# One of the two softmax rows per four that TensorE turned goes through a DMA turn: window attention heads of a hybrid encoder layer

## Chip, cores and metric

The kernel runs on one core of a Trainium2 chip. The metric is the device time of one execution in microseconds (us). The time before is 1037.27 us, the median of 3 runs (1036.99 to 1037.58).

## What is computed

One encoder layer over 1024 tokens of width 1024, in float32. One normed input feeds one projection; eight "A" heads do sliding-window attention with a learned sink, eight "B" heads do neighbourhood attention on a 16 x 64 grid; both are normed, joined and projected out; then a gated MLP and a last norm. The change is in the A heads alone, whose core in the reference is, per block of 128 queries and a span of 384 keys:

```
s = einsum('bqgrd,bkgd->bgrqk', q_i, k_i) * scale
s = where(valid, s, -1e30)
m = maximum(max(s, axis=-1), sink_gr)
p = exp(s - m[..., None])
denom = sum(p, axis=-1) + exp(sink_gr - m)
o = einsum('bgrqk,bkgd->bgrqd', p, v_i) / denom[..., None]
```

There are 2 key/value heads (g) with 4 query heads each (j = 0 to 3) and 8 query blocks (b).

## The kernel before

**Stages.** The projections of the input are made as jobs: each is a chain of products of 128x512 (L172, L173, L174: high part by high, low by high, high by low). While the first jobs run, their q, k and v are split into high and low parts and stacked. Then attention runs as 48 units, 16 for the A heads (two g times eight b, `unit_window`) and 32 for the B heads (`units_grid`). The remaining jobs are poured in between as filler, so TensorE always has products to do beside the attention. After attention come the output projection and the MLP.

**A softmax row.** "Row" here is the 128 queries of one block of one head, with 256 keys at the two ends of the sequence and 384 elsewhere. It goes through `Rows.softmax`: GpSimd copies the sink beside the scores (L461), VectorE adds the mask, moves the scores out of PSUM and finds the maximum (L462), ScalarE takes the exponential and the sum (L466), VectorE the reciprocal (L467). After that the row must be split into a high and a low float16 part and turned, because the product with v (L521) needs keys on the partitions. A letter of `PATH_A` says how, for j = 0, 1, 2, 3:

- D: ScalarE writes the high part (L481) and VectorE the low part (L483) into a staging buffer, and a DMA on SyncE's queue turns both at once (L488).
- P: GpSimd scales the row (L470), ScalarE writes the high part (L476), GpSimd subtracts for the low part (L477), and the same DMA turns both (L488).
- T: GpSimd scales the row (L470), TensorE turns it in blocks of 128x128 into a PSUM bank named pt (L494), ScalarE copies the high part out of that bank (L497) and VectorE makes the low part from it (L498).

`PATH_A` was "DPTT". The staging buffers are three, `hl` and two pieces of `stage`, taken in turn (`staged`). A T row stays in its `p` buffer, of which there are five, until TensorE turns it; the bank pt has two buffers. The turned rows of two heads share one `Rows` tile, and the six products of a unit with v (L521) read first the tile of j = 0 and 1, then that of j = 2 and 3.

**What sets the order.** TensorE's order is written by hand: in unit u the scores of unit u + 2 (L432), the products of unit u with v (L521) and the turns of the T rows of unit u + 1 (L494) form one list of events. `T_NEXT` says at which places of that list the turns are put in, `T_AT` does so for the T rows of unit 0, and `T_B` for the B heads. Behind every event the filler is given a share of its rate divided by the number of events, `per = RATES[wi] / (8 if u < 16 else 4) / len(events)`; the shares are summed as a float in `debt`, and `fill(int(debt))` pours in so many steps of filler. The other engines' orders come from a scheduler that works from priorities.

Of the kernel before, what the change touches and what calls it, by code (L numbers as in the profile page):

```python
# [37 lines left out]
TURNED, PS, HLS, SPARE_A, LOWS = 3, 5, 1, (2, 5), 1  # L38
LEAD = 3
BIAS0, YS = 8, 1  # L40
T_AT = (0, 4)
PATH_A, PATH_B = "DPTT", ["QQTQQQTQ"] * 8
T_B, T_NEXT = (0, 3), (3,8)
SPARE_B = [(1, 3), (1, 3), (3,), ()]
WARM = 10

# [17 lines left out]
def hybrid_layer(tc, xT, w_in, w_out, w_gate, w_up, w_down, small, sink, rpb, consts, rope, out):  # L64
    nc = tc.nc
    with ExitStack() as ctx:
# [890 lines left out]
        for u in range(len(flat)):  # L957
# [8 lines left out]
            if u == 0:  # L966
                for i, w in enumerate(flat[u][4]):
                    events.insert(T_AT[i], ("v", w))
            if u + 1 < len(flat):
# [918 lines left out]
```

## Time and profile before

| | |
|---|---|
| median of 3 runs | 1037.27 us |
| span of the profiled execution, first to last instruction | 1035.9 us |
| what the median has beyond that span | 1.3 us |
| TensorE busy | 1011.7 us (98%) |
| VectorE, ScalarE, GpSimd busy | 880.0, 679.3, 214.1 us |
| window attention on TensorE, about | 62 to 191 us |
| grid attention, about | 191 to 350 us |

Times in rows are in us from the span's start. A row of the timeline has the start, the duration, the engine, the line and the operation; what stands in brackets is how long the engine had been idle ahead of it, and who released it. PE is TensorE, PEld its loading of weights, DVE VectorE, ACT ScalarE, POOL GpSimd, SPq the queue of SyncE. The time before one execution's first instruction and behind its last is not in the trace; the table takes it as the difference of median and span.

### The profile page before, as it was taken

What the parts mean: (1) busy time and instruction counts of PE and PEld (TensorE: products, weight loads), DVE (VectorE), ACT (ScalarE), POOL (GpSimd) and SP (SyncE); (2) the same over time, 40 slices, a digit from 0 to 9 for tenths busy, and PEclk for the clock granted to TensorE, in tenths of its full rate; (3) what the DMA queues carried; (4) which work ended last, traced back from release to release, by engine and by line L of the source; (5) the groups of instructions that cost most, each with busy time, mean ns of one, the idle gap of its engine ahead of it and who ended that gap; (6) DMA issues with size and microseconds to landing.
All of it is one profiled execution on the core that took longest, in us unless ns stands there. A gap on an engine that the chain in (4) does not pass through costs nothing.

```text
span 1035.9 us, 15696 instructions
## 1 busy us (share of the span) xinstructions
PE 1011.7 (98%) x5102; PEld 577.3 (56%) x5102; DVE 880.0 (85%) x1748; ACT 679.3 (66%) x1243; POOL 214.1 (21%) x341
## 2 busy tenths in 40 slices
PE   9998999999999999999999999999999999999996
PEld 7776777777775545544444444444444444444446
DVE  6699998766898699899898988888888879899875
ACT  8567787767687587645777777754535656655551
POOL 2235455676866301000000000000000000000002
PEclk9999999999999999999999999999999999999998
DMA  9447473676689775300687867733232778878744
GB/s 347 155 98 149 109 139 83 151 168 140 134 180 224 213 276 193 121 1 21 222 266 261 276 241 250 251 111 133 82 112 102 240 252 297 301 250 264 255 153 163
DMA packets 144275, 191.28 MB, mean 185 GB/s; under 512 B 77376, under 2 KB 88640, under 8 KB 144192
## 3 DMA queue, kind: packets, MB, share of 16 engines
q1 hardware_dynamic: 133536, 164.51, 54.7%
q10 hardware_dynamic: 10656, 25.76, 6.4%
q8 instruction: 40, 0.66, 0.2%
q14 instruction: 43, 0.35, 0.1%
HBM read 132.81 MB, written 28.57 MB: 156 GB/s over the span
## 4 chain that ended last, share of the span: by engine, by line
PE 71%; DVE 6%; ACT 1%; DMA 1%; issue 1%; POOL 0%; ACTq 0%; DVEq 0%; SPq 0%; POOLq 0%
PE dn L1177 6%; PE dn L1178 6%; PE dn L1176 6%; PE pj L180 6%; PE z L1176 5%; PE z L1177 5%; PE z L1178 5%; PE y L1176 4%; PE y L1177 4%; PE y L1178 4%; PE x L1176 4%; PE x L1177 4%; PE x L1178 3%; PE pj L172 2%; PE pj L174 2%; PE pj L173 2%
## 5 line engine op out<-in xcount | busy, mean ns | idle before, releaser
L1178 PEld LDWEIGHTS <-wlo 128*128 128x128 f16 x898 | 87.9, 98 | 101.3 <-DVE wlo L1151 0.2
L1176 PEld LDWEIGHTS <-whi 128*128 128x128 f16 x898 | 88.1, 98 | 100.3
L1177 PEld LDWEIGHTS <-whi 128*128 128x128 f16 x898 | 87.9, 98 | 100.3 <-issue 0.2
L1178 PE MATMUL dn<-xd,wlo 128*128 128x512 f16 (+1 forms) x330 | 120.4, 365 | 0.0
L1177 PE MATMUL dn<-xd,whi 128*128 128x512 f16 (+1 forms) x330 | 120.4, 365 | 0.0
L1176 PE MATMUL dn<-xd,whi 128*128 128x512 f16 (+1 forms) x330 | 120.4, 365 | 0.0
L172 PE MATMUL pj<-xgh,whi 128*128 128x512 f32 x248 | 106.8, 431 | 0.8 <-ACT whi L156 0.8
L1177 PE MATMUL z<-hg,whi 128*128 128x512 f16 x264 | 100.1, 379 | 0.0
L1178 PE MATMUL z<-hg,wlo 128*128 128x512 f16 x264 | 100.1, 379 | 0.0
L1176 PE MATMUL z<-hg,whi 128*128 128x512 f16 x264 | 100.1, 379 | 0.0
L466 ACT ACTIVATE p<-p,nm 128x385 f32<-128x385 f32 (+3 forms) x128 | 74.8, 585 | 38.0 <-DVE nm L462 33.3
L174 PE MATMUL pj<-xgh,wlo 128*128 128x512 f32 x248 | 97.9, 395 | 1.4 <-POOL wlo L157 1.4
L173 PE MATMUL pj<-xgl,whi 128*128 128x512 f32 x248 | 97.5, 393 | 0.0
L1150 ACT ACTIVATE whi<-ws,m 128x512 f16<-128x512 f32 (+1 forms) x96 | 65.9, 709 | 35.6 <-DVE ws L1317 19.5
L1151 DVE SCALAR_TENSOR_TENSOR wlo<-ws,m,whi 128x512 f16<-128x512 f32 (+1 forms) x96 | 70.2, 741 | 17.8 <-ACT whi L1150 17.6
L1031 POOL TENSOR_TENSOR back<-back,cst 128x4 f32<-128x4 f32 (+1 forms) x7 | 2.8, 396 | 356.7 <-DVE back L1030 356.7
L1165 ACT ACTIVATE scan<-scan 128x1024 f32<-128x1024 f32 (+1 forms) x60 | 61.1, 1019 | 17.0 <-DMA scan<-in_w_down_dram 12.3
L1150 ACT ACTIVATE whi<-raw,m 128x512 f16<-128x512 f32 (+1 forms) x78 | 51.4, 700 | 17.9 <-DMA raw<-in_w_down_dram 12.7
L1151 DVE SCALAR_TENSOR_TENSOR wlo<-raw,m,whi 128x512 f16<-128x512 f32 (+1 forms) x78 | 55.4, 732 | 7.5 <-ACT whi L1150 6.9
L1176 PE MATMUL y<-hg,whi 128*128 128x512 f16 x160 | 60.6, 379 | 0.0
L1177 PE MATMUL y<-hg,whi 128*128 128x512 f16 x160 | 60.6, 379 | 0.0
L1178 PE MATMUL y<-hg,wlo 128*128 128x512 f16 x160 | 60.6, 379 | 0.0
(291 smaller groups left out, 2465.5 us busy)
## 6 DMA issues: line engine op xcount, KB each, us to landing
xd<-x SPq DMA_DIRECT2D x77, 256.0 KB, 5.4
raw<-in_w_down_dram SPq DMA_DIRECT2D x64, 256.0 KB, 3.8
x<-c ACTq DMA_DIRECT2D x22, 512.0 KB, 3.5
scan<-in_w_gate_dram SPq DMA_DIRECT2D x18, 512.0 KB, 4.7
scan<-in_w_up_dram SPq DMA_DIRECT2D x18, 512.0 KB, 4.3
raw<-in_w_gate_dram SPq DMA_DIRECT2D x18, 512.0 KB, 3.8
raw<-in_w_up_dram SPq DMA_DIRECT2D x18, 512.0 KB, 4.4
raw<-in_w_in_dram SPq DMA_DIRECT2D x32, 256.0 KB, 3.1
```

The costliest lines, as they stand in the source:

```text
L172: nc.tensor.matmul(ps, w[0], x[0][:, tsl(h)], start=first, stop=False)
L173: nc.tensor.matmul(ps, w[0], x[1][:, tsl(h)], start=False, stop=False)
L174: nc.tensor.matmul(ps, w[1], x[0][:, tsl(h)], start=False, stop=last)
L180: nc.tensor.matmul(ps, a, b, start=i == 0 and b is x[h][0] and a is w[0], stop=i == len(ws) - 1 and a is w[1])
L466: nc.scalar.activation(p[:, 0:e], p[:, 0:e], AF.Exp, bias=nm, scale=-1.0, accum_out=sm)
L1031: nc.gpsimd.tensor_tensor(back, back, unit_back.to_broadcast([128, n]), op=ALU.mult)
L1150: mark["whi"] = nc.scalar.activation(hi, src, AF.Copy, scale=by)
L1151: nc.vector.scalar_tensor_tensor(lo, src, by, hi, op0=ALU.mult, op1=ALU.subtract)
L1165: nc.scalar.activation(t, t, AF.Square, accum_out=dst)
L1176: nc.tensor.matmul(ps, w[0], x[0], start=first and i == 0, stop=False, skip_group_check=True)
L1177: nc.tensor.matmul(ps, w[0], x[1], start=False, stop=False, skip_group_check=True)
L1178: nc.tensor.matmul(ps, w[1], x[0], start=False, stop=last and i == len(ws) - 1, skip_group_check=True)
```

## The change

Head j = 2 goes the way of P in place of T, and the tables of places lose the entry of the turn that is gone. The constants feed every unit of the A heads; nothing else is edited.

```diff
-T_AT = (0, 4)
-PATH_A, PATH_B = "DPTT", ["QQTQQQTQ"] * 8
-T_B, T_NEXT = (0, 3), (3,8)
+T_AT = (4,)
+PATH_A, PATH_B = "DPPT", ["QQTQQQTQ"] * 8
+T_B, T_NEXT = (0, 3), (8,)
```

TensorE, at the first unit of the A heads, before; pt is the bank a row is turned into, p the row, o the output, s the scores, pj a projection.

```order
L494 MATMUL pt_855<-cst_89,p_765 128x128 x3
L521 LDWEIGHTS v_466
L521 MATMUL o_833<-turned_610,v_466 128x256
L521 LDWEIGHTS v_466
L521 MATMUL o_833<-turned_610,v_466 128x256
L172 MATMUL pj_783<-xgh_281,whi_701 128x512
L173 MATMUL pj_783<-xgl_282,whi_701 128x512
L174 MATMUL pj_783<-xgh_281,wlo_702 128x512
L494 MATMUL pt_866<-cst_89,p_671 128x128 x2
L432 MATMUL s_871<-ka_538,q_545 128x384
```

The same place on TensorE now.

```order
L521 LDWEIGHTS v_466
L521 MATMUL o_834<-turned_610,v_466 128x256
L521 LDWEIGHTS v_466
L521 MATMUL o_834<-turned_610,v_466 128x256
L432 MATMUL s_858<-ka_538,q_545 128x384
L432 MATMUL s_858<-kb_539,q_545 128x384
L172 MATMUL pj_789<-xgh_281,whi_704 128x512
L173 MATMUL pj_789<-xgl_282,whi_704 128x512
L174 MATMUL pj_789<-xgh_281,wlo_705 128x512
L494 MATMUL pt_875<-cst_89,p_674 128x128 x2
```

The turn of the next unit's j = 2 (p_765) is gone; the turn of this unit's j = 3 (p_671, now p_674) is left, and it stands behind the scores that it stood ahead of.

GpSimd over the same rows, before; hl and stage are the staging buffers.

```order
L470 TENSOR_SCALAR p_652<-p_652,sm_654 128x256
L470 TENSOR_SCALAR p_671<-p_671,sm_673 128x256
L364 COPY up_727<-up_727 64x1
L350 TENSOR_TENSOR gains_121<-par_79,up_727 128x1 x2
L461 COPY p_793<-nsink_168 128x1
L470 TENSOR_SCALAR p_714<-p_714,sm_716 128x384
L477 TENSOR_TENSOR hl_622<-p_714,hl_622 128x3x128
```

GpSimd now.

```order
L470 TENSOR_SCALAR p_652<-p_652,sm_654 128x256
L470 TENSOR_SCALAR p_674<-p_674,sm_676 128x256
L477 TENSOR_TENSOR stage_621<-p_652,stage_621 128x2x128
L461 COPY p_799<-nsink_168 128x1
L364 COPY up_730<-up_730 64x1
L350 TENSOR_TENSOR gains_121<-par_79,up_730 128x1 x2
L461 COPY p_841<-nsink_168 128x1
L470 TENSOR_SCALAR p_717<-p_717,sm_719 128x384
L477 TENSOR_TENSOR stage_621<-p_717,stage_621 128x3x128
```

The subtraction for j = 2 (p_652) has come in between, and the copies, scalings and subtractions of the following rows stand behind it. SyncE's queue has one more L488 per unit, between the loads of weights and the moves of q, k and v.

TensorE in the B heads, late (a turn of the sixth head), before; mg is the normed mix that the output projection reads.

```order
L180 LDWEIGHTS whi
L180 MATMUL pj<-mg,whi 128x512
L180 LDWEIGHTS whi
L180 MATMUL pj<-mg,whi 128x512
L180 LDWEIGHTS wlo
L180 MATMUL pj<-mg,wlo 128x512
L494 MATMUL pt<-cst,p 128x128 x3
L596 LDWEIGHTS v
L596 MATMUL o<-turned,v 128x256
```

The same turn now.

```order
L494 MATMUL pt<-cst,p 128x128 x3
L180 LDWEIGHTS whi
L180 MATMUL pj<-mg,whi 128x512
L180 LDWEIGHTS whi
L180 MATMUL pj<-mg,whi 128x512
L180 LDWEIGHTS wlo
L180 MATMUL pj<-mg,wlo 128x512
L596 LDWEIGHTS v
L596 MATMUL o<-turned,v 128x256
```

One step of filler (three products) has passed from ahead of the turn to behind it. Nothing of the B heads is edited: the sum in `debt` now comes from eleven events a unit where there were twelve, it lands on the other side of a whole number, and the step comes out one event later. The same stands at some other turns of the later B heads.

## The prediction

> **What bounds the kernel now.** I read the page's busy times first, then the table by stage, then what ended last.
>
> ```profile
> PE 1011.7 (98%) x5102; PEld 577.3 (56%) x5102; DVE 880.0 (85%) x1748; ACT 679.3 (66%) x1243; POOL 214.1 (21%) x341
> PEclk9999999999999999999999999999999999999998
> PE 71%; DVE 6%; ACT 1%; DMA 1%; issue 1%; POOL 0%; ACTq 0%; DVEq 0%; SPq 0%; POOLq 0%
> core 0: us, PE busy (x) PEld busy (x) DVE busy (x) ACT busy (x) POOL busy (x), PEclk, DMA share, GB/s
> 76.00:191.00 115.00, 110.27 (x631) 82.79 (x629) 104.08 (x347) 88.46 (x226) 57.04 (x120) 1.00 0.60 123
> 191.00:350.00 159.00, 155.34 (x877) 114.33 (x877) 121.64 (x359) 115.05 (x256) 114.63 (x144) 1.00 0.78 161
> ```
>
> TensorE is busy 98% of the span at a full granted clock, and the chain that ended last is mostly its own. In the window attention (the row 76:191) it is busy 110.3 of 115 us. But VectorE is close behind with 104.1 us, ScalarE has 88.5, GpSimd only 57.0, and the DMA engines are busy six tenths of it. So in this stage TensorE's work and its waits set the time, VectorE has about 10% of room, and what the change hands to GpSimd and DMA lands where there is room. After this stage TensorE's order is full of products to the end, so what it gains here should pass through.
>
> **What the removed turn costs TensorE.** Matmuls overlap, so their durations say too much; I take the starts.
>
> ```profile
> 97.67 0.39 PE L174 MATMUL pj<-xgh,wlo 128*128 128x512 f32 x1
> 97.90 0.33 PE L432 MATMUL s<-ka,q 128*128 128x384 f32 x1
> 98.07 0.34 PE L432 MATMUL s<-kb,q 128*128 128x384 f32 x1
> 98.95 0.40 PE L174 MATMUL pj<-xgh,wlo 128*128 128x512 f32 x1
> 99.18 0.49 PE L494 MATMUL pt<-cst,p 128*128 128x128 f32 x3
> 99.43 0.42 PE L432 MATMUL s<-ka,q 128*128 128x384 f32 x1
> 99.69 0.34 PE L432 MATMUL s<-kb,q 128*128 128x384 f32 x1
> 125.42 0.38 PE L494 MATMUL pt<-cst,p 128*128 128x128 f32 x2
> 125.56 0.36 PE L432 MATMUL s<-ka,q 128*128 128x256 f32 x1
> ```
>
> Without a turn the scores start 0.23 us after the product ahead of them (97.67 to 97.90), and the second score matmul 0.17 later. With three turned blocks in between it is 0.48 (98.95 to 99.43) and 0.26: the turn takes 0.25 us and makes the next matmul 0.09 later, 0.34 together. Two blocks take 0.14 (125.42 to 125.56), with the same 0.09 some 0.23. There are 16 turns less, 12 of three blocks and 4 of two (the ends of the sequence, twice): 12 x 0.34 + 4 x 0.23 = 5.0 us. If the 0.09 is hidden, it is 12 x 0.25 + 4 x 0.14 = 3.6.
>
> **The waits ahead of the turns.** In the window attention the turns are also where TensorE stands still.
>
> ```profile
> L494 PE MATMUL pt<-cst,p 128*128 128x128 f32 x88 | 15.2, 277 | 3.7 <-DVE turned L498 1.3 <-POOL p L470 1.3 <-POOL p L461 1.1
> 80.19 0.44 PE L494 MATMUL pt<-cst,p 128*128 128x128 f32 x2 [1.31 <-DVE turned L498]
> 95.56 0.52 PE L494 MATMUL pt<-cst,p 128*128 128x128 f32 x3 [1.08 <-POOL p L461]
> 118.20 0.55 PE L494 MATMUL pt<-cst,p 128*128 128x128 f32 x3 [0.34 <-POOL p L470]
> 163.10 0.55 PE L494 MATMUL pt<-cst,p 128*128 128x128 f32 x3 [0.41 <-POOL p L470]
> 179.69 0.55 PE L494 MATMUL pt<-cst,p 128*128 128x128 f32 x3 [0.52 <-POOL p L470]
> ```
>
> The five sum to the 3.7 us of the group. Turns alternate between j = 2 and j = 3; by their order, the last four are all j = 2, the turn that goes. They waited for GpSimd's scaling of that row. The first (80.19) is j = 3 of the first unit, waiting for VectorE to empty the bank pt; two turns of j = 2 had just filled both banks, and these go as well. So I take off all 3.7 us, with 0 as the other bound if the next thing is as late.
>
> What is late next would be the turn of j = 3. It had room:
>
> ```profile
> 148.12 0.59 POOL L470 TENSOR_SCALAR p<-p,sm 128x384 f32<-128x384 f32 x1
> 150.87 0.49 PE L494 MATMUL pt<-cst,p 128*128 128x128 f32 x3
> L477 POOL TENSOR_TENSOR stage<-p,stage 128x384 f16<-128x384 f32 x8 | 7.4, 920 | 2.3 <-ACT stage L476 2.1
> L477 POOL TENSOR_TENSOR stage<-p,stage 128x256 f16<-128x256 f32 x3 | 2.0, 675 | 0.5 <-ACT stage L476 0.5
> ```
>
> Its row was ready 2.2 us before its turn (148.71 to 150.87). GpSimd now has one subtraction more per unit, 0.92 us, on the same queue and ahead of this row's scaling in most units, so the row is later by about that; and TensorE comes sooner. On the other side the turn itself stands one event later. I let this row wait as the other did in steady units: 1.08 + 0.34 + 0.41 + 0.52 = 2.35 us of new waits. The bounds are 0 and 16 x 0.92 = 14.7.
>
> **What moves to other engines.**
>
> ```profile
> L498 DVE TENSOR_TENSOR turned<-pt,turned 128x384 f16<-128x384 f32 x24 | 13.0, 553 | 2.2 <-ACT turned L497 2.0
> L497 ACT ACTIVATE turned<-pt 128x384 f16<-128x384 f32 x24 | 11.2, 480 | 0.6 <-PE pt L494 0.5
> L476 ACT ACTIVATE stage<-p 128x384 f16<-128x384 f32 x8 | 4.2, 525 | 3.3 <-POOL p L470 3.2
> L461 POOL COPY p<-nsink 128x1 f32<-128x1 f32 x59 | 16.2, 278 | 33.3 <-PE pt L494 15.2 <-DVE stage L483 9.8 <-DVE hl L483 7.3
> L488 SPq DMA_TRANSPOSE turned<-stage x21: 1198/1222/1922, 67.6 to 185.6; - x21
> turned<-stage SPq DMA_TRANSPOSE x21, 2.8
> ```
>
> None of these is on the path while TensorE has work. VectorE loses 16 subtractions of up to 0.553 us, at most 8.8 us. ScalarE trades a copy of 0.480 for one of 0.525: 16 x 0.045 = 0.7 us more. GpSimd gains 12 x 0.92 + 4 x 0.675 = 13.7 us. If the stage shrinks by some 7 us to 108, the shares are VectorE 95.3 / 108 = 88%, ScalarE 89.2 / 108 = 83%, GpSimd 70.7 / 108 = 65%: no engine overtakes TensorE. The p buffer of j = 2 is freed sooner: GpSimd stood 15.2 us in front of L461 because TensorE had not yet turned a row; that works for the change. SyncE's queue issues 16 turns more at 1.22 us, 19.5 us, and each lands 2.8 us after its issue. Its order puts them ahead of loads of weights and moves of q, k and v; a unit takes about 7.5 us, a row of unit u + 2 is made during unit u, so this row has two units (15 us) until its product. Cost: nothing, as long as that cover holds. On the other DMA side, a load that comes one turn (1.2 us) later is still a whole job ahead.
>
> **The later turns.** The order of filler around some turns of the B heads moves by one step of three products, and one such turn already waited:
>
> ```profile
> 312.64 0.38 PE L180 MATMUL pj<-mg,wlo 128*128 128x512 f16 x1
> 314.04 0.55 PE L494 MATMUL pt<-cst,p 128*128 128x128 f32 x3 [1.02 <-POOL p L470]
> 311.99 0.38 PE L180 MATMUL pj<-mg,wlo 128*128 128x512 f16 x1
> ```
>
> A step is 0.65 us (311.99 to 312.64). This turn now comes that much sooner for a row that GpSimd is not done with: +0.65. The other turns that move had no wait; bounds: 0, and 7 x 0.65 = 4.6 if all seven that I count lacked room.
>
> **The sum**, against the profiled span of 1035.9 us: -5.0 (turns) - 3.7 (waits) + 2.35 (new waits) + 0.65 (B heads) = -5.7, so 1030.2. The median of the runs is 1.3 above that span, so I forecast 1031.5 us.
>
> **Rivals.**
>
> *No new waits (0.16).* The free p buffers and the idler VectorE bring every row sooner, and j = 3 keeps its room. Then -5.0 - 3.7 + 0.65 and nothing else: 1029.2; with a similar gain at the B heads' turns instead of the loss, 1028.
>
> *GpSimd's queue becomes late (0.14).* If the subtraction delays each remaining turn by half its 0.92 us, the new waits are 16 x 0.46 = 7.4 in place of 2.35: 1036.5. For it: j = 2 had four waits on this engine. Against: GpSimd at 65%, and the 2.2 us of room. It decides when the row of j = 3 is later by over 2.2 us.
>
> *VectorE becomes the bound (0.06).*
>
> ```profile
> 74.81 1.11 POOL L477 TENSOR_TENSOR hl<-p,hl 128x384 f16<-128x384 f32 x1 [0.64 <-ACT hl L476]
> 75.05 1.42 DVE L157 TENSOR_TENSOR wlo<-raw,whi 128x512 fp32r<-128x512 f32 x1
> L157 DVE TENSOR_TENSOR wlo<-raw,whi 128x512 fp32r<-128x512 f32 x11 | 8.3, 754 | 0.1
> ```
>
> Beside a GpSimd subtraction VectorE's split of weights took 1.42 us where the mean is 0.754. If each of the 16 new subtractions costs VectorE 0.67 us, that is 10.7, more than the 8.8 it loses; the stage stays near 106 us of VectorE work and nothing is gained: about 1037. [...]
>
> *Slower: the DMA turn is the slow way (0.12).*
>
> ```profile
> 74.20 0.53 ACT L476 ACTIVATE hl<-p 128x384 f16<-128x384 f32 x1 [1.39 <-POOL p L470]
> 75.95 1.21 SPq L488 DMA_TRANSPOSE turned<-hl  x1
> ```
>
> Three rows per unit now share three staging buffers, so each buffer must be written, subtracted, issued and read within one unit. In these rows that takes from 74.20 to 75.95 and 2.8 more, 4.6 us, of a unit that shrinks to about 7. If SyncE's queue, which issues in order, adds over 2.4 us, ScalarE stands in front of a full buffer with the next rows' exponentials behind it, and TensorE runs out of rows. One us lost in each of the 14 later units gives 1037.3 - 5.0 - 3.7 + 0.65 + 14 = 1043.2. Against it: no wait for a staging buffer in the window attention before. [...]
>
> **Chances and range.** Forecast 0.50, the rivals 0.16, 0.14, 0.06 and 0.12, the rest (0.02) unknown. About 0.2% (2 us) is what a measurement of this kernel can tell from no change. Faster by more: the forecast, the first rival and the milder part of the second (0.10): 0.76. Within it: the rest of the second, the third, and a little: 0.12. Slower: 0.12. The range goes from the first rival (1028.0) over the forecast to the second and third (1037.3), and leaves out the slow case.
>
> **What would show it.** In the profile after: 44 L494 of the window attention instead of 88; the idle time ahead of them at 1 to 3 us; unit spacing near 7.1 us; GpSimd's idle time for TensorE ahead of L461 halved; no ScalarE wait for a DMA at L476 or L481. I am wrong if TensorE waits at L521 for a DMA, if L494 waits for L470 in most units, or if the B heads' turns give back more than 2 us.

## The result, and the profile after

The kernel with the change takes 1040.66 us (median of 8 runs, 1038.42 to 1043.57), the kernel before on the same chip 1037.67 (8 runs, 1036.83 to 1038.82): a ratio of 1.0025, interval 1.0014 to 1.0036. It is slower by some 2.6 us, where 6 us less were forecast, and it lies outside the range (1028.0 to 1037.3). The profiled execution took 1043.35 us, one of the longest of the eight, with a span of 1041.6 against 1035.9 before.

To see in which stage the time goes, I take three marks on TensorE in both profiles: the first scores (start of the window attention), the first and the last product of the B heads. These are the rows of the kernel before, then of the kernel after.

```profile
62.29 0.28 PE L432 MATMUL s<-ka,q 128*128 128x256 f32 x1
197.53 0.39 PE L596 MATMUL o<-turned,v 128*128 128x256 f16 x2
353.05 0.38 PE L596 MATMUL o<-turned,v 128*128 128x256 f16 x2
```

```profile
64.92 0.28 PE L432 MATMUL s<-ka,q 128*128 128x256 f32 x1
199.61 0.27 PE L596 MATMUL o<-turned,v 128*128 128x256 f16 x1 [0.27 <-DMA turned<-stage]
356.79 0.27 PE L596 MATMUL o<-turned,v 128*128 128x256 f16 x1
```

The window attention went from 135.24 to 134.69 us, half a microsecond less where 6.4 were forecast (all of the sum but the B heads' 0.65). The B heads went from 155.52 to 157.18. The rest of the 5.7 us is ahead of the attention (2.6) and behind the B heads (2.0). TensorE's order is the same ahead of the first scores; other profiles of this study, with that order too, have them between 62.13 and 63.81, so I take most of the 2.6 for scatter between executions, and judge by medians below. The profile after shows where it lies: near 20 us TensorE waits 1.76 us ahead of L172 where it waited 0.56 before, and behind that the granted clock is 0.83, 0.50 and 0.81 in three stretches of 2 us, 1.7 us of work lost. None of the other 18 profiles has a slow clock there.

The clock is no small part of the medians either. The mean granted clock of an execution was 0.992 to 0.995 after (the eight runs, middle value 0.993) and 0.995 to 0.998 before (26 runs beside e1 to e4, middle value between 0.996 and 0.997). Over the span that is an estimated 7.3 us lost after and 3.6 before, from clocks given to a thousandth, which is 1 us: as much as the whole difference of the medians, or more.

In the window attention, the turns did what was said: fewer of them, and no wait ahead of them. The groups at the turn and at the product with v, for the stage 76 to 191 us, after; the row of L521 before follows, since it was not shown.

```profile
L494 PE MATMUL pt<-cst,p 128*128 128x128 f32 x42 | 7.2, 278 | 0.0
L521 PE MATMUL o<-turned,v 128*128 128x256 f16 x162 | 30.4, 279 | 6.5 <-ACT turned L497 4.0 <-DVE mixa L536 2.4 <-DVE turned L498 0.2
```

```profile
L521 PE MATMUL o<-turned,v 128*128 128x256 f16 x165 | 30.7, 277 | 0.9 <-DVE mixa L536 0.6 <-DVE by L480 0.2
```

The stage's row after, for VectorE's share:

```profile
76.00:191.00 115.00, 107.89 (x589) 80.48 (x587) 98.79 (x330) 88.69 (x225) 70.56 (x135) 0.99 0.76 144
```

VectorE is busy 98.8 of 115 us, 86%. It has less to do than before (104.1), near the 88% that was expected, and yet, as the rows below show, it is what TensorE waits for.

Ahead of the turns TensorE no longer stands at all: 3.7 us before, 0.0 now. But it stands 6.5 us ahead of L521 where it stood 0.9. The largest of these waits is in the first unit. TensorE, then VectorE, then ScalarE, and the table by 2 us behind it:

```profile
80.96 0.38 PE L494 MATMUL pt<-cst,p 128*128 128x128 f32 x2
85.31 0.27 PE L521 MATMUL o<-turned,v 128*128 128x256 f16 x1 [3.98 <-ACT turned L497]
```

```profile
81.18 1.82 DVE L375 SCALAR_TENSOR_TENSOR vhl<-t,down,vhl 64x1024 f16<-64x1024 f32 x1
83.03 0.62 DVE L462 CUSTOM_DVE_ANT_0 p<-s,cst,nsink 128x384 f32<-128x384 f32 x1
```

```profile
83.69 0.62 ACT L466 ACTIVATE p<-p,nm 128x385 f32<-128x385 f32 x1 [2.98 <-DVE nm L462]
84.90 0.36 ACT L497 ACTIVATE turned<-pt 128x256 f16<-128x256 f32 x1
```

```profile
core 0: us, PE busy (x) PEld busy (x) DVE busy (x) ACT busy (x) POOL busy (x), PEclk, DMA share, GB/s
82.00:84.00 2.00, 0.00 (x0) 0.00 (x0) 1.97 (x4) 0.31 (x1) 1.16 (x2) 1.00 0.80 194
84.00:86.00 2.00, 0.50 (x3) 0.32 (x3) 1.53 (x8) 1.94 (x7) 0.59 (x1) 1.00 0.86 131
86.00:88.00 2.00, 2.00 (x9) 1.39 (x8) 0.71 (x2) 0.44 (x1) 1.17 (x3) 0.54 0.53 109
88.00:90.00 2.00, 2.00 (x9) 1.56 (x9) 1.14 (x5) 1.07 (x4) 0.01 (x1) 0.60 0.88 87
```

The releaser that the row names, ScalarE's copy L497, is not the cause. It was ready to run at 81.3, but stood on ScalarE's queue behind exponentials (L466) that waited for VectorE's maximum (L462), and this stood on VectorE's queue behind the split of v (L375, 1.82 us; 1.28 in the same place before). So the lateness was handed on from queue to queue: the wait of 3.98 us is named after the last link, and its root, the 1.82 us of L375, is two engines back. Behind it the granted clock was 0.54 and 0.60 for 4 us, another 1.7 us of work lost (2 x 0.46 + 2 x 0.40). The last section has shorter stands behind which the clock fell too.

So the stage adds up: -5.0 (turns) - 3.7 (waits at the turns) + 5.6 (waits at L521) + 1.7 (clock) = -1.4, against -0.55 measured. With 0.4 us of waits at L432 and the 0.27 ahead of the first L596 it is -0.7.

In the B heads the moved step is at 314 us in the profile before, here at 318. TensorE, GpSimd, and the table by 2 us:

```profile
313.98 0.38 PE L180 MATMUL pj<-mg,wlo 128*128 128x512 f16 x1
317.92 0.58 PE L494 MATMUL pt<-cst,p 128*128 128x128 f32 x3 [3.56 <-POOL p L470]
```

```profile
313.78 1.43 POOL L554 TENSOR_TENSOR xb<-cst,rr 128x384 f32<-128x384 f32 x1
...
316.31 1.55 POOL L470 TENSOR_SCALAR p<-p,sm 128x384 f32<-128x384 f32 x1
```

```profile
318.00:320.00 2.00, 2.00 (x8) 1.02 (x9) 0.94 (x2) 1.39 (x3) 1.74 (x4) 0.57 1.07 278
320.00:322.00 2.00, 2.00 (x9) 1.19 (x8) 0.28 (x1) 0.00 (x0) 1.82 (x3) 0.58 1.02 135
```

The turn waits 3.56 us instead of 1.02, on a GpSimd that makes the next head's bias (L554, and L555 behind it) ahead of the scaling (L470), and again TensorE runs at 0.57 and 0.58 for 4 us behind it.

### The profile page after: what moved, and what is told of

It is laid out like the page before. It is cut to its first block, busy times and chain, and to the rows that moved or that the text cites. A ratio compares the mean times of both kernels' runs of the same rounds, so it can differ in the third digit from the quotient of the medians.

```text
span 1041.6 us, 15641 instructions
## 1 busy us (share of the span) xinstructions
PE 1011.6 (97%) x5058; PEld 575.2 (55%) x5058; DVE 873.3 (84%) x1732; ACT 678.6 (65%) x1243; POOL 229.0 (22%) x357
## 4 chain that ended last, share of the span: by engine, by line
PE 60%; DVE 10%; DMA 6%; ACT 3%; issue 3%; POOL 1%; SPq 0%; DVEq 0%; ACTq 0%; POOLq 0%
PE pj L180 8%; PE z L1176 5%; PE z L1177 5%; PE z L1178 5%; PE x L1176 3%; PE y L1176 3%; PE x L1177 3%; PE y L1177 3%; PE y L1178 3%; PE x L1178 3%; DMA xd<-x 2%; PE dn L1177 2%; PE dn L1176 2%; PE dn L1178 2%; DVE xd L1581 2%
## 5 line engine op out<-in xcount | busy, mean ns | idle before, releaser
L172 PE MATMUL pj<-xgh,whi 128*128 128x512 f32 x248 | 108.2, 436 | 0.6 <-ACT whi L156 0.6
L174 PE MATMUL pj<-xgh,wlo 128*128 128x512 f32 x248 | 98.5, 397 | 1.4 <-POOL wlo L157 1.4
L466 ACT ACTIVATE p<-p,nm 128x385 f32<-128x385 f32 (+3 forms) x128 | 74.8, 585 | 31.3 <-DVE nm L462 30.2
```

The costliest lines, as they stand in the source:

```text
L172: nc.tensor.matmul(ps, w[0], x[0][:, tsl(h)], start=first, stop=False)
L174: nc.tensor.matmul(ps, w[1], x[0][:, tsl(h)], start=False, stop=last)
L466: nc.scalar.activation(p[:, 0:e], p[:, 0:e], AF.Exp, bias=nm, scale=-1.0, accum_out=sm)
```

## The experiments

Every ratio is against the kernel before, timed on the same chip beside it. The experiments ran on four chips, a question at a time, so kernels of different questions are compared by their ratios. Waits come from the one profile of a kernel, and one execution is not the median: e3's is the fastest of its twelve.

**First question: which part costs?** One edit moves the first turn of j = 3 back by one event, away from its own product; another gives the sum `debt` the value that it has in the kernel before, so that TensorE's order in the B heads is that of before.

e1, the turn alone:

```diff
-T_AT = (4,)
+T_AT = (3,)
```

> The changed kernel with the first unit's one turn put one event earlier (place 3 in place of 4), so that a product step and the scores stand between the turn and the product that reads it. Theory 1 (the loss is two stalls: the first unit's turn stands right ahead of its own product, and the moved filler step in the B heads): the wait of 4.2 us at L521 near 81 us falls under 1 us and the slow clock of 0.54 to 0.60 behind it (about 1.7 us lost) goes, so 5 to 6 us less than the changed kernel: 1034.5 to 1036. Rival (the way over GpSimd and DMA is itself slower, the place does not matter): about 1040.7, as the changed kernel.

Measured: 1043.15 us, ratio 1.0046 (1.0032 to 1.0060).

e2, the order of the B heads alone:

```diff
-            wi = u // 8 if u < 16 else 2 + (u - 16) // 4
+            wi = u // 8 if u < 16 else 2 + (u - 16) // 4; debt = 0.9999999999999971 if u == 16 else debt
```

> The changed kernel with the filler's carried sum set at the first unit of the B heads to the value that the kernel before has there, so that TensorE's order in the B heads is that of before. Theory 1: the wait at the turn near 314 us falls from 3.7 to about 1.2 us and the slow clock behind it goes (1.7 us): about 4 us less than the changed kernel, 1036.5. Rival (A heads only): within 1 us of 1040.7.

Measured: 1038.80 us, ratio 1.0004 (0.9994 to 1.0013).

e3, both edits:

> Both edits of the two kernels ahead of this one. Theory 1: the gains add, 9 to 10 us less than the changed kernel: 1031 to 1032, the sum of the prediction. Rival (GpSimd and DMA way is slower): 1038 to 1041, not faster than the kernel before.

Measured: 1039.40 us, ratio 1.0018 (1.0007 to 1.0028).

e4, the kernel before with the B heads' order of the kernel after:

```diff
-            wi = u // 8 if u < 16 else 2 + (u - 16) // 4
+            wi = u // 8 if u < 16 else 2 + (u - 16) // 4; debt = 0.9999999999999949 if u == 16 else debt
```

> The kernel before, its filler's carried sum set at the first unit of the B heads to the value of the changed kernel, so that only the order in the B heads is the changed one. Theory 1: slower than before by 0.65 us (the step alone) to 4 us (if the wait passes the length at which the clock falls): 1038.3 to 1041.7. Rival (the late row in the B heads came from what the change does upstream): 1037.7, as before.

Measured: 1041.15 us, ratio 1.0029 (1.0018 to 1.0040). Its wait at that turn is 3.54 us, for the same L470, and the granted clock behind it 0.63 and 0.51 in two stretches of 2 us (318 to 322 us). The 4 us of the expectation suppose a length of wait at which the clock falls; no run shows a fixed one (last section).

e2 and e4 agree: the step that a rounding moved in the B heads is worth 2 to 3 us (0.0021 between after and e2, 0.0029 between e4 and before). With it out of the way, the change in the window attention is worth nothing (e2: 1.0004), not 6 us. The theory on the first turn's place fell: in e3 that wait became shorter (2.58 us in place of 3.98), and the kernel no faster (e1 1.0046 against 1.0025 after, e3 1.0018 against 1.0004 in e2). The waits came back further on. TensorE's waits in e3, 62 to 200 us (engine, tile, line waited for: us in total, times, longest):

```profile
PE o L521 <- DVE mixa L536: 4.6, 3, 2.6
PE o L521 <- DVE turned L498: 2.8, 2, 2.6
PE s L432 <- DVE nm L462: 1.3, 3, 0.6
```

VectorE is named in every one of them. One of the waits for mixa, the emptying of the o bank: TensorE, ScalarE, then VectorE's queue.

```profile
95.05 0.39 PE L521 MATMUL o<-turned,v 128*128 128x256 f16 x2 [2.56 <-DVE mixa L536]
```

```profile
89.27 0.38 ACT L532 ACTIVATE ot<-o 64x256 f32<-64x256 f32 x1
```

```profile
89.28 1.22 DVE L341 TENSOR_TENSOR kb<-t,ka 64x1024 fp32r<-64x1024 f32 x1
90.42 0.60 DVE L483 SCALAR_TENSOR_TENSOR hl<-p,by,hl 128x384 f16<-128x384 f32 x1
...
91.58 0.55 DVE L498 TENSOR_TENSOR turned<-pt,turned 128x384 f16<-128x384 f32 x1
92.05 0.68 DVE L269 TENSOR_TENSOR t<-pj,rstd 128x512 f32<-128x512 f32 x1
92.64 1.22 DVE L299 SCALAR_TENSOR_TENSOR t<-t,q 128x1024 fp32r<-128x1024 f32 x1
...
94.49 0.50 DVE L536 TENSOR_TENSOR mixa<-o,ot 64x128 f32<-64x128 f32 x2
```

ScalarE's half of the bank was done at 89.65, and no row of VectorE between 89.28 and 94.49 has a wait: L536 stood 4.8 us behind other work. Theory 2: VectorE, which takes its work in the order of its queue, is as late as TensorE, so what TensorE saves it waits for VectorE. Rival: GpSimd's added subtractions, by their queue or by contention (in the profile after an L157 on VectorE took 1.41 us beside GpSimd's L477, the median of eleven is 0.683).

**Second question: VectorE or GpSimd?** e5 moves the low part of the weights (L157) from VectorE to GpSimd; e6 does it to the kernel before; e7 leaves out GpSimd's new subtraction; e8 gives it to VectorE.

e5, on e3:

```diff
-            if u == 12:
+            if u == 0:
                 mark["attention"] = True
```

> The kernel of e3 (j = 3 turned one event earlier, B heads' filler in the old order; its median was 1039.4 us), and from the first attention unit on the low part of the weights (L157) is made by GpSimd, where before that starts with the thirteenth unit. That takes some 11 operations of 0.75 to 0.88 us, 8 to 10 us, off VectorE in the window attention and gives GpSimd about as much. Theory (VectorE's in-order queue is as late as TensorE in the window attention, so that what TensorE saves it waits at the products with v, L521, and the scores, L432): VectorE's results come sooner, TensorE's waits at L521 for VectorE's mixa (L536) and turned (L498) shrink from the 5 to 6 us of e3 to 2 to 3, and the median is 1033 to 1036. Rival (GpSimd's queue and its contention with VectorE eat the gain): GpSimd, at 70.6 of 115 us after the change, gets later still, two-input VectorE work is slowed more, and the median is 1040 to 1045, with waits for POOL in the place of those for VectorE.

Measured: 1042.51 us, ratio 1.0037 (1.0022 to 1.0051).

e6, the same edit on the kernel before:

> The kernel before with the same move of the weights' low part (L157) to GpSimd from the first unit, as control for e5. Theory (VectorE late): before the change TensorE's waits in the window attention were 6.3 us in large ones, 4.1 of them the first turn and GpSimd's; VectorE has most of its late work in the first three units, so the move helps before as well, but less than after: 1035.5 to 1038. Rival (GpSimd late): GpSimd's scaling, which the turns of j = 2 waited for, comes later, and the median is 1039 to 1043.

Measured: 1038.11 us, ratio 0.9996 (0.9986 to 1.0006).

e7, on e3 (j counts within a pair of rows here, so that the one meant is j = 2; the buffers are cleared once ahead):

```diff
-                        nc.gpsimd.tensor_tensor(lo, x, hi, op=ALU.subtract)
+                        if j: nc.gpsimd.tensor_tensor(lo, x, hi, op=ALU.subtract)
```

> The kernel of e3 with the low part of the DMA-turned row of j = 2 left out: GpSimd's subtraction L477 for that row is not made (the three staging buffers are set to zero once), so that the row's low part is not that of the reference. 16 GpSimd operations of 0.68 to 0.92 us, 13.7 us, are gone, with all their contention; VectorE keeps all its work. Theory (VectorE's own queue): VectorE's operations in the window attention get 1.6 us shorter at most (what e3 showed them to be longer by), and the median is 1037.5 to 1039.5, little better than e3 (1039.4). Rival (GpSimd's subtractions eat the gain, by its queue or by contention): the whole gain that was forecast comes back, 1031 to 1034.

Measured: 1041.83 us, ratio 1.0033 (1.0018 to 1.0049).

e8, on e3:

```diff
-                        nc.gpsimd.tensor_tensor(lo, x, hi, op=ALU.subtract)
+                        (nc.gpsimd if j else nc.vector).tensor_tensor(lo, x, hi, op=ALU.subtract)
```

> The kernel of e3 with the subtraction of j = 2's row made by VectorE instead of GpSimd: 16 operations of 0.5 to 0.6 us, some 9 us, go back to VectorE, about what it lost with L498. VectorE has then the load of before (104 us in the window attention) and GpSimd too (57), while TensorE has 16 turns less. Theory (VectorE late): TensorE's waits for VectorE at L521 and L432 grow by some 4 to 8 us against e3, and the median is 1042 to 1047. Rival (GpSimd's queue or contention): GpSimd's results come sooner, and the median is 1032 to 1037, below e3.

Measured: 1044.76 us, ratio 1.0058 (1.0043 to 1.0072). TensorE's waits:

```profile
PE o L521 <- DVE mixa L536: 7.5, 3, 4.2
PE o L521 <- DVE turned L498: 2.8, 2, 2.4
PE s L432 <- DVE nm L462: 2.6, 3, 1.6
```

e7 rules the new subtractions out as the cause: with 16 of them gone, and their contention too, nothing came back. It even came out 2.3 us above what theory 2 had expected, which is open. e8 is as theory 2 has it: with VectorE's work back the kernel is 4 us slower than e3, and the waits for VectorE in its profile are 12.9 us in these three rows, 8.7 in e3. The operation itself got shorter by the move (0.58 us on VectorE, 0.98 on GpSimd in e3, for 128x384), so it is VectorE's queue that costs here, not the length of this row's chain. But e5 missed: VectorE had less to do, and the kernel was slower than e3; the same move in the kernel before (e6) changed nothing. GpSimd's ten L157 in e5 (62 to 192 us) take 1.29 us each, 12.9 us in the queue in which the scalings stand; so e5 took load off one engine and put more on another. A cleaner cut was needed.

**Third question: less work for VectorE, and none for others.** e9 leaves out VectorE's low part of the first row, e10 does so in the kernel before. e11 and e12 are on e3 and try the two other explanations: the staging buffers, and L536's place in the queue.

e9, on e3 (buffers cleared once; lines behind stand 2 further down, so L521 is L523):

```diff
                         if path == "D":
-                            nc.vector.scalar_tensor_tensor(lo, x, by, hi, op0=ALU.mult, op1=ALU.subtract)
+                            if nsink is None: nc.vector.scalar_tensor_tensor(lo, x, by, hi, op0=ALU.mult, op1=ALU.subtract)
```

> The kernel of e3 with the low part of the first row (j = 0) left out: VectorE's L483 is not made in the window attention (the three staging buffers are set to zero once), so that this row's low part is not that of the reference. 16 VectorE operations of 0.5 to 0.76 us, some 11 us of 132, are gone, and nothing takes their place; GpSimd and DMA keep what they had in e3. Theory (VectorE's in-order queue is what TensorE waits for once the turns are gone): TensorE's waits at L521 for mixa (L536) and turned (L498), 7.4 us in e3, fall to 2 to 4, and the median is 1033 to 1036. Rival (the DMA turn with its three staging buffers, or GpSimd): no less wait, 1038 to 1041.

Measured: 1035.17 us, ratio 0.9963 (0.9949 to 0.9976).

e10, the same edit on the kernel before:

> The kernel before with the same L483 left out, as control for e9: the first row's low part is not that of the reference. Theory (VectorE late): before the change TensorE waits for turns, which VectorE's queue feeds too, so this gains as well, but TensorE's own turns stay: 1035 to 1037, and e9 is below it by 1 to 4 us, the worth of the 16 turns. Rival: 1037.5 to 1039, no change, and e9 no better than it.

Measured: 1036.80 us, ratio 0.9984 (0.9974 to 0.9994).

e11, on e3 (every fourth row takes the buffer y):

```diff
+            turns_of["a"] = turns_of.get("a", 0) + 1
+            if sink and turns_of["a"] % 4 == 0:
+                stage.insert(0, stage.pop())
+                return apool.tile([128, 3, 2, 128], F16, name="y", tag="y", bufs=YS)
             return stage[-1]
```

> The kernel of e3 with four staging buffers for the DMA turns of the window attention instead of three (the fourth is the buffer y, which only the B heads use). In e3 ScalarE waited 2.1 us in four places (L481, L476) for a DMA to have read its staging buffer, and before the change nowhere. Theory (VectorE late): ScalarE's waits for DMA go, TensorE's waits for VectorE stay; the median is 1038 to 1040, within 1 us of e3. Rival (the DMA turn's buffers, the slower case of the prediction): the median falls by 2 us or more against e3, to 1034 to 1037.

Measured: 1039.82 us, ratio 1.0011 (1.0001 to 1.0021).

e12, on e3, in `leave`:

```diff
+                with tc.high_priority(offset=60):
                     for e in range(2):
```

> The kernel of e3 with the emptying of the o bank (ScalarE's L532, VectorE's L536) given priority in the scheduler, so that it stands ahead of other queued work. In e3 the largest waits of TensorE were at L521 for that bank: 4.6 us in three places, in one of which (92.1 to 95.05 us) the two L536 were ready and stood behind 4.8 us of other VectorE work. Theory (VectorE late): if only the place in the queue is at fault, the waits for mixa go to under 1.5 us and the median is 1034.5 to 1036.5; if VectorE's whole load is, they go over to other waits for VectorE (nm L462 at the scores, turned L498), and the median stays at 1038 to 1041. I hold the second for the likelier. Rival (DMA turn or GpSimd): 1038 to 1041 with waits for POOL or DMA.

Measured: 1040.30 us, ratio 1.0011 (1.0001 to 1.0021). TensorE's waits:

```profile
PE s L432 <- DVE nm L462: 3.6, 4, 1.3
PE o L521 <- DVE turned L498: 2.6, 1, 2.6
```

The waits for mixa are gone, and the scores wait for VectorE's maximum instead: the place of this one operation in the queue was not at fault. e11 shows no gain from a fourth buffer. e9 gained 5.5 thousandths on e3 (1.0018 to 0.9963), 5.7 us, while the same cut before gained 1.7 (0.9984): this work of VectorE is worth some three times as much once the turns are gone. In e9's waits for VectorE little is left:

```profile
PE o L523 <- ACT turned L499: 1.9, 1, 1.9
PE o L523 <- DVE mixa L538: 1.6, 2, 1.3
PE s L432 <- DVE nm L464: 0.4, 2, 0.2
```

**Fourth question: load, or the chain of the first row?** GpSimd's L461 and the DMA turn wait for L483, so e9 cut a chain as well as a load. e13 puts the load back without the chain. e14 and e15 look for a complete kernel without that load.

e13, on e9:

```diff
+                        if path == "D" and nsink is not None:
+                            y = apart(mark["scratch"][:, 0:n])
+                            eye = bass.AP(tensor=ident.tensor, offset=ident.offset, ap=[list(ident.ap[0]), [0, c], [1, 128]])
+                            nc.vector.scalar_tensor_tensor(y, eye, by, y, op0=ALU.mult, op1=ALU.subtract)
```

> The kernel of e9 (the first row's low part, L483, left out, so that it is not that of the reference), and in the place of each L483 a VectorE operation of the same form and size on constant data into a spare piece of memory: it waits for nothing but VectorE's own by (L480), and nothing waits for it. VectorE has the load of e3 again; GpSimd, ScalarE and the DMA turns have what they had in e9. Theory (VectorE's load in its in-order queue): the waits at L521 come back, and the median is 1038 to 1041. Rival (the place of L483 in the chain of the row: GpSimd's L461 and the DMA turn waited for it): no change against e9, 1034 to 1036.5.

Measured: 1043.39 us, ratio 1.0045 (1.0033 to 1.0057). With the load back e9's gain is gone, and more: e13 stands 8 us above e9, where e3 stood 5.7. But it is no clean test of the load. Its longest wait on TensorE, and VectorE ahead of it (L528 is L521 here, L504 is L497):

```profile
82.64 0.83 PE L528 MATMUL o<-turned,v 128*128 128x256 f16 x2 [3.48 <-ACT turned L504]
```

```profile
78.08 1.06 DVE L287 TENSOR_TENSOR f<-f,turns 128x128 f32<-128x128 f32 x2 [1.24 <-DMA f<-t]
```

VectorE, with two of its 16 added operations done by then, stood idle for a DMA, and the maximum that ScalarE and then TensorE waited for stood behind that. SyncE's queue had issued this DMA (L285) at 74.54 us behind four DMA turns of this stage; in e3 it went out at 73.14 behind three, and VectorE did not wait there. The clock fell behind the stand of 3.48 us (mean granted clock 0.86 from 76 to 100 us, where e3 has 1.00), and 3.4 us were lost between 80 and 90 us. Wait and clock are 6.9 us, where e3 has a wait of 2.58 and a full clock: 4.3 of the 5.2 us between the two profiled spans. So the scheduler, run anew, gave an order with one more cost in it, and e13 agrees with VectorE's load as the cause without showing it alone. e9 has the DMA wait as well (0.88 us).

e14, on e3, and e15, on the kernel before:

```diff
-PATH_A, PATH_B = "DPPT", ["QQTQQQTQ"] * 8
+PATH_A, PATH_B = "PPPT", ["QQTQQQTQ"] * 8
```

```diff
-PATH_A, PATH_B = "DPTT", ["QQTQQQTQ"] * 8
+PATH_A, PATH_B = "PPTT", ["QQTQQQTQ"] * 8
```

> The kernel of e3 with the first row (j = 0) sent the way P too (PATH_A PPPT): its low part is made by GpSimd (L470, L477) and not by VectorE (L483, L480). Everything is computed. VectorE loses 16 L483 and 16 L480, some 12 us; GpSimd gains 16 scalings and 16 subtractions, some 22 us, and comes to about 92 of 115 us. Theory (VectorE's load): VectorE's waits go as in e9, but GpSimd at 80% is late now and then: 1035 to 1038. Rival (GpSimd's queue late): 1041 to 1046, with waits for POOL.

Measured: 1049.76 us, ratio 1.0102 (1.0084 to 1.0119), with GpSimd at 82.1 us of the 115 and VectorE at 84.2.

> The kernel before with the first row sent the way P (PATH_A PPTT): the same load taken off VectorE, given to GpSimd, and all turns kept. GpSimd comes to about 79 of 115 us. Theory (VectorE's load): a little faster than before, as e10 (1036.8), less what GpSimd's scaling comes later for the turns: 1036 to 1039. Rival (GpSimd's queue late): 1039.5 to 1043.

Measured: 1040.38 us, ratio 1.0018 (1.0009 to 1.0027). TensorE's largest wait in e15:

```profile
PE pt L494 <- POOL p L470: 5.0, 4, 2.4
```

My forecast for e14 was wrong by 12 us, and that for e15 by over 1; both went the way of the rival. In e15 work that went from VectorE to GpSimd made GpSimd's scalings late (5.0 us where it was 1.3 before), long before GpSimd is busy all the time. In e14 I take it for the same, but its profile doesn't show it: that execution was the fastest of six by 5 us, and its largest wait on TensorE is for VectorE's maximum (7.8 us at L432).

**Fifth question: the change where VectorE has room.** VectorE's load isn't even. The kernel before, by 24 us:

```profile
76.00:100.00 24.00, 21.29 (x121) 15.55 (x119) 22.31 (x67) 18.12 (x44) 11.95 (x24) 1.00 0.75 148
100.00:124.00 24.00, 23.66 (x141) 18.01 (x139) 22.68 (x76) 18.36 (x48) 13.22 (x28) 1.00 0.52 120
124.00:148.00 24.00, 23.25 (x131) 17.38 (x130) 22.42 (x78) 18.97 (x51) 11.25 (x27) 1.00 0.67 129
148.00:172.00 24.00, 23.59 (x135) 17.83 (x135) 20.59 (x68) 19.11 (x48) 11.66 (x27) 1.00 0.47 86
```

VectorE (the fifth column) is busy 93 to 95% up to 148 us, and 86% behind that. e16 and e17 make the change in the last 8 and the last 5 window units alone, with the B heads' order of before; the edit is e17's, without the lines that hand each unit its own path, and e16 has 8 and 8 in place of 11 and 5.

```diff
-PATH_A, PATH_B = "DPTT", ["QQTQQQTQ"] * 8
+PATH_A, PATH_B = ["DPTT"] * 11 + ["DPPT"] * 5, ["QQTQQQTQ"] * 8
...
-                    events.insert((T_NEXT if u < 15 else T_B)[i], ("v", w))
+                    at = T_NEXT[2 - len(flat[u + 1][4]):] if u < 15 else T_B
+                    events.insert(at[i], ("v", w))
```

> The kernel before with the change made in the last 8 of the 16 window units alone (the second key/value head, from about 128 us), turn positions as after the change in those units and as before in the first 8, and the filler of the B heads in the order of before. 8 turns less on TensorE: 6 x 0.34 + 2 x 0.23 = 2.5 us at most. Theory (VectorE's load, which is lower in the later units): some of the saving comes through, 1036 to 1038. Rival (the turn's saving never comes through, since the rows' chain by GpSimd and DMA is later): 1038 to 1040.

Measured: 1037.45 us, ratio 0.9992 (0.9982 to 1.0001).

> As e16, in the last 5 window units alone (from about 150 us, where VectorE was busy 9.4 to 10.6 of 12 us before). 5 turns less on TensorE: 4 x 0.34 + 0.23 = 1.6 us at most, and one wait of 0.4 and one of 0.5 us ahead of turns of j = 2 gone. Theory: 1036.5 to 1038, no slower than before. Rival: 1038 to 1039.5.

Measured: 1035.14 us, ratio 0.9973 (0.9963 to 0.9982). It computes everything and is faster than both kernels, by 2.8 us against before and by more than I had expected. The waits in its profile:

```profile
PE o L521 <- DVE mixa L536: 1.7, 2, 1.1
PE pt L494 <- DVE turned L498: 1.3, 1, 1.3
PE pt L494 <- POOL p L461: 1.1, 1, 1.1
```

The two waits of 0.41 and 0.52 at the turns of 163 and 179 us are gone, and 5 turns, 1.6 us: 2.5 us. Against it stand 1.1 us of new waits for mixa (1.7, 0.6 before), so that the 2.8 measured are more than these rows account for. Eight units did not do better than five. That fits the rows above, where VectorE is at 93% from 128 to 148 us, but nothing else was tried on it.

## Why the prediction was wrong, point by point

- **The turns' price (5.0 us)** held as TensorE's work: 42 turned blocks in the stage instead of 88, their busy time 7.2 us instead of 15.2, and the stage's sum closes with it to 0.2 us. Where VectorE had room (e17) the kernel became faster.
- **The waits at the turns (-3.7 + 2.35)** failed, and this is the step that cost the forecast. I asked what is late next, and looked for it in one place, the remaining turn, which has 0.0 us of wait. What was late next was VectorE, and its lateness shows at L521 and L432: 6.5 us at L521 instead of 0.9. The sum had no term for this, and none for the slow clock behind a long stand, 1.7 us here. That VectorE's queue is the cause is shown by the two waits followed back, and by e8 and by e9 against e10: work added to it cost (e8 1.0058, e3 1.0018), work taken off it gained (e9 0.9963), and gained more than before the change (e10 0.9984). How much of it is load alone, and how much the place of that work in the rows' chains, stays open, since e13 brought a cost of its own.
- **"No engine overtakes TensorE"** is the sentence behind it. I took VectorE's share over the whole stage (104.1 of 115, then an expected 88%) as room. The share itself came out nearly right, 86%, and room it was not. Before, in the first 72 us, it is 93 to 95%, and each row passes VectorE several times, in order, in turn with ScalarE; one operation in its queue at the wrong time, L375 at 81.18 with its 1.82 us, was at the root of the wait of 3.98. The stage table that I read was too coarse to show it.
- **The rival on VectorE (0.06)** named the right engine and the time (about 1037 without the B heads), with the wrong mechanism. Its mechanism was contention with GpSimd, which it read from a pair of rows (L157 1.42 us beside L477; the median of the eleven is 0.686). Other rows before bear such a price out for some operations and not for others: L328 took 1.74 us at 197.09, beside GpSimd's L157 and L487, where the median of the sixteen is 0.92, but L498 at 101.47, beside L477, took 0.55, the mean of the 24 of its form. No run shows 0.67 us for each new subtraction, and e7, without them, is no faster than e3, so contention did not decide here.
- **GpSimd late (0.14)** did not happen: no L494 in the stage waits for L470, and e7 agrees. It does happen when GpSimd gets still more on top of two turns (e15, 5.0 us at L494 for L470).
- **The slow DMA turn (0.12)** had the right sign, but not the mechanism. ScalarE did wait for a DMA, 2.1 us in the stage, where I had listed none:

```profile
L481 ACT ACTIVATE hl<-p,by 128x384 f16<-128x384 f32 x11 | 6.7, 608 | 1.9 <-DMA turned<-hl 1.4 <-ACT p L466 0.5
L476 ACT ACTIVATE stage<-p 128x256 f16<-128x256 f32 x6 | 2.5, 417 | 2.4 <-POOL p L470 1.7 <-DMA turned<-stage 0.7
```

A fourth buffer (e11) brought nothing that stands out, so these waits were mostly off the path. The prediction also put at nothing that the new DMA turns stand ahead of moves of q and k on SyncE's queue; in the window attention of the kernel after no operation waits for such a move, but in e13 it is the start of the longest wait.

- **The B heads (+0.65)** had the right place and mechanism and the wrong size: 2 to 3 us. The step's length was added, while GpSimd's scaling came later too (1.55 us long, where the one at 148.12 us before took 0.59) and 4 us of slow clock came behind. By my own bound of 2 us I had named this as what would prove me wrong.

What stays open: the last 0.9 us between e13 and e3, why e7 is above its forecast, and why e17 gains more than its rows account for.

## What to carry to other kernels

Before work is taken off the busiest engine, read the second busiest by short stretches, not over the stage: where it was above 90% here (93 to 95%), the gain turned into waits for it, at instructions that had next to no wait before (6.5 us at L521, 0.9 before), and moving its work to a third engine, GpSimd, brought no gain that stands out in any of four kernels (e5 1.0037 and e14 1.0102 on e3's 1.0018, e6 0.9996, e15 1.0018). Follow a named releaser back through the queues it stood in. Where a change lets a planner run again, compare the order far from the edit too: a rounding there cost 2 to 3 us here, while the change in the window attention brought nothing.

## What was not expected of the hardware

- In the kernel after, stands of TensorE of 3.98 and 3.56 us cost almost half as much again: the granted clock was 0.54 to 0.60 for the 4 us behind them (86 to 90 us, 318 to 322 us), 1.7 us each. A shorter one cost it too in some executions and not in others. Near 62 us all 19 profiles have a wait of 1.35 to 1.38 us ahead of L174, with a shorter wait some 2 us earlier; in 11 of them the clock fell behind it to 0.50 for some 3.5 us, in 8 it stayed at 1.00 (before, with 1.38 us, and after, with 1.36, at 1.00; in e15, with 1.36, the products behind it start 0.43 us apart until 65.07 us and 0.23 later). In e3 the wait of 2.56 us that ended at 95.05 left the clock at 1.00; in e7 one of 2.55 at the same place did not (0.71, 0.50 and 0.94 in the 2 us stretches from 94 to 100 us). The stretch behind it, e3 and then e7:

```profile
96.00:98.00 2.00, 2.00 (x13) 1.39 (x12) 1.34 (x7) 1.50 (x4) 1.67 (x3) 1.00 0.98 191
```

```profile
96.00:98.00 2.00, 2.00 (x8) 1.32 (x7) 1.32 (x7) 1.49 (x5) 0.77 (x2) 0.50 1.09 189
```

- The same GpSimd scaling (L470) of 128x384 took 0.59 us in one place (148.12 us, before) and 1.55 in another (316.31 us, after), and the split of weights (L157) 0.754 us on VectorE (before, mean of eleven) and 1.287 on GpSimd (e5, mean of ten).
